# A two-layer decoder trunk: other seven-product units in the MLP, half-block loads, and pinned loads and forms

## The chip, the cores and the metric

The kernel runs on one core of one Trainium2 chip. The metric is the device time of one execution in microseconds (us). The kernel before took 2167.83 us (median of 3 runs, 2164.54 to 2170.95).

The core has a matrix engine (TensorE, PE in the profile; PEld is its weight load), a vector engine (VectorE, DVE), a scalar engine (ScalarE, ACT), GpSimd (POOL) and the sync engine (SyncE, SP), whose queue issues most DMAs. Each engine works through its own queue in order and waits on semaphores.

## The reference

Two layers (`DEPTH = 2`) act on x of 256 rows (tokens) by 2048 columns, in float32. Only the second half of a layer, the MLP, is touched by the change:

```
x  = x + concat([A, Cv]) @ w_out[l]          # attention and short convolution
hm = rmsnorm(x, mlp_norm_g[l]) @ w_up[l]     # 2048 -> 8192
x  = x + square(relu(hm)) @ w_down[l]        # 8192 -> 2048
```

## The kernel before, in words

**Precision.** A float32 product is made of three products in a faster format: each operand is cut into a high part (`hi`) and a low part (`lo = x - hi`), and hi·hi, hi·lo and lo·hi are summed in PSUM. So each weight tile that arrives by DMA is first worked on by ACT (`whi`, `uhi`, lines 291 and 719) and then by DVE (`wlo`, `ulo`, lines 292 and 720), each on 128x1024 elements.

**Pass 1 of the MLP** (lines 908 to 951) goes over 32 units of 256 hidden columns. For unit i it makes the up product in two columns c, each in two halves kh of the contraction (`up_part`, L856), takes the result out of PSUM (`evict`: ACT `ev` L866, DVE L867), squares it (`square`), and two units later (`LAG = 2`) multiplies it with two blocks of rows of `w_down` for the *left* 1024 output columns. That down product is a 2x2 block product done with seven products instead of eight (L904), which needs sums of the blocks: on the side of the activations four sums S1 to S4 (`in_forms`, L890 to L896), on the side of the weights differences `t` (L754, L757, L758), and hi and lo parts of all (L740, L741: `b1`, `b2`, `t13`, `t24`). I call the weight side the forms of a unit. The raw down weights of a pair come into the tile `draw` (pool `dpool`, 2 buffers, line 727); the `t`, `b2`, `t13` and `t24` tiles have one buffer each, `b1` two.

**Pass 2** (from line 1003) makes the *right* 1024 output columns from stored activations. Twelve units, listed in `SEVEN`, go through seven products again: 21 matmuls, and all their forms. The twenty others (`PLAIN`) go through the ordinary product (L1060): 24 matmuls, with two weight tiles of hi and lo (k = 0 and 1). Plain units' activations were written to DRAM in pass 1 with their hi and lo parts (`plain`, L883) and come back two units at a time as a block `g` (line 955, GpSimd's queue) into one of four buffers that the normalized input `nT` of pass 1 had. The seven-product units' activations (`hid`, L879) come back one at a time into the tile `h` (L806; one buffer) and are summed again.

**What sets the order.** TensorE's order is the program's (`manual_schedule`). Weight tiles are *jobs*; `Weights.take` traces jobs up to three ahead of the product that uses them (`AHEAD = 3`), in an order that `mlp` writes out by hand: in pass 2 the four jobs of a seven-product unit (b1 and b2; t13; the activation sums f; t24) are hung behind jobs of the plain units in front of it (lines 828 to 843). The queues of ACT, DVE, POOL and SP are filled by a planner that works with its own estimates of time: an instruction may stand anywhere that its data and buffers allow. `late(...)` pins an instruction behind what was traced before it on its engine.

**Places that the change touches:** the list `SEVEN` (line 36); the wait of 5 ticks in `Norm.factors` (line 460) before the matmul `rbc` that spreads the norm's ratio (line 462; a tick is a fixed step in the matmul stream, one per four up matmuls); `load_rows` (line 724); `quarters` (line 732), whose `keep` pins the forms of unit 0 in pass 1; the order of jobs (line 830); unit 0 of pass 1, whose two columns share one PSUM tile `up0` of two banks (line 913); `block`, `block(0)`, `block(1)` and the first `load_again` (lines 953 to 959); the place of `block(b + 2)` in pass 2 (line 1039).

## Time and profile before

| | us |
|---|---|
| median of 3 runs | 2167.83 |
| lowest, highest | 2164.54, 2170.95 |
| the profiled execution | 2165.76 |
| its span (first to last instruction) | 2164.0 |
| TensorE busy in the span | 2136.1 |
| VectorE busy | 1710.8 |
| ScalarE busy | 1300.9 |

In layer 0, pass 1 begins at 395.8 us of the span, pass 2 at 912.4, and the next layer's mixer at about 1086; in layer 1, pass 1 begins at 1469.7 and pass 2 at 1984.9.

How to read it: the view of waits says which engine stood idle for whom. A timeline line has start, duration, engine, line of the kernel, operation, output tile and inputs, and in brackets the idle time just before it and who ended it. A window line has its bounds and length and then, for each engine, busy time and instructions, the granted TensorE clock, the share of time the DMA engines moved data, and their GB/s. A busy engine is not an engine at its peak: DVE operations overlap a little at their ends, so that the spacing of starts is the better price.

### The profile page before, as it was taken

The page shows a single profiled execution, that of the slowest core. Times are in us where ns is not written, and L with a number is a line of the kernel's source. Part 1 is how long each engine was busy: PE and PEld are TensorE (multiplying, and loading weights), DVE is VectorE, ACT ScalarE, POOL GpSimd, SP SyncE. Part 2 cuts the span into 40 slices and gives each one's busy share as a digit, 9 for nine tenths or more (in the row PEclk, how much of TensorE's full clock was granted, in tenths as well). Part 3 has the DMA queues.
Part 4 walks back from the last instruction along what each step waited for, and adds up shares of the span by engine and source line. Part 5 has one row for each costly group of instructions (what it writes and reads, how often), then busy time and mean ns, then how long its engine had stood idle before and what let it go on. Part 6 is the DMA issues. An engine that isn't in the chain of part 4 may idle for free.

```text
span 2164.0 us, 29108 instructions
## 1 busy us (share of the span) xinstructions
PE 2136.1 (99%) x10966; PEld 1812.7 (84%) x10966; DVE 1710.8 (79%) x2397; ACT 1300.9 (60%) x1760; POOL 166.2 (8%) x246
## 2 busy tenths in 40 slices
PE   9999999999999999999999999999999999999999
PEld 7888888888888888788788888888888888887877
DVE  5677655698888888799866776557988888887997
ACT  6556445566666666656565664446666666665554
POOL 3021200000000000000001222000000000000000
PEclk9999999999999999999999999999999999999999
DMA  7655766587767777887565557656777767778873
GB/s 256 183 158 166 236 187 188 160 263 217 227 216 231 224 224 223 272 288 275 188 184 176 156 166 245 186 172 196 253 227 219 224 216 232 222 224 274 310 271 108
DMA packets 285534, 467.62 MB, mean 216 GB/s; under 512 B 10611, under 2 KB 191429, under 8 KB 282832
## 3 DMA queue, kind: packets, MB, share of 16 engines
q1 hardware_dynamic: 268128, 413.17, 61.2%
q0 software_dynamic: 17216, 52.56, 7.0%
q8 instruction: 86, 1.41, 0.3%
q14 instruction: 56, 0.46, 0.1%
q10 hardware_dynamic: 48, 0.02, 0.0%
HBM read 436.32 MB, written 29.38 MB: 215 GB/s over the span
## 4 chain that ended last, share of the span: by engine, by line
PE 85%; DVE 7%; DMA 4%; issue 2%; ACT 1%; POOL 1%; DVEq 0%; POOLq 0%; ACTq 0%
PE upc L856 30%; PE pr L904 13%; PE o L361 8%; PE rt L1060 5%; PE gb L383 4%; PE v L361 4%; PE ci L383 4%; PE gc L383 4%; PE rt L904 3%; PE q L361 3%; PE k L361 3%; DVE wlo L292 2%; DMA draw<-in_w_down_dram 1%; DMA h<-hid 1%; PE upw L856 1%
## 5 line engine op out<-in xcount | busy, mean ns | idle before, releaser
L291 ACT ACTIVATE whi<-raw 128x1024 fp32r<-128x1024 f32 (+1 forms) x338 | 355.6, 1054 | 410.6 <-PE rt L1060 87.8
L292 DVE TENSOR_TENSOR wlo<-raw,whi 128x1024 fp32r<-128x1024 f32 (+1 forms) x338 | 414.4, 1229 | 237.3 <-ACT whi L291 232.7
L856 PE MATMUL upc<-nT,uhi 128*128 128x512 f32 x1920 | 477.6, 391 | 0.0
L719 ACT ACTIVATE uhi<-uraw 128x1024 fp32r<-128x1024 f32 x256 | 271.2, 1060 | 288.1 <-PE upc L856 254.2
L856 PEld LDWEIGHTS upc<-nT,uhi 128*128 128x128 f32 x1920 | 352.8, 188 | 68.2
L720 DVE TENSOR_TENSOR ulo<-uraw,uhi 128x1024 fp32r<-128x1024 f32 x256 | 313.0, 1223 | 115.7 <-ACT uhi L719 113.3
L856 PEld LDWEIGHTS upc<-nT,ulo 128*128 128x128 f32 x1920 | 261.9, 190 | 18.7
L856 PE MATMUL upc<-nT,ulo 128*128 128x256 f32 x1920 | 267.7, 282 | 0.0
L1060 PE MATMUL rt<-whi,g 128*128 128x512 f32 x608 | 194.0, 393 | 0.0
L361 PE MATMUL o<-whi,cat 128*128 128x512 f32 x512 | 159.6, 390 | 0.0
L1060 PEld LDWEIGHTS rt<-whi,g 128*128 128x128 f32 x608 | 115.7, 190 | 24.1
L1060 PE MATMUL rt<-wlo,g 128*128 128x512 f32 x304 | 120.3, 396 | 9.4 <-DVE wlo L292 9.2
L361 PEld LDWEIGHTS o<-whi,cat 128*128 128x128 f32 x512 | 96.1, 188 | 19.7
L754 DVE TENSOR_TENSOR t<-draw 128x1024 f32<-128x1024 f32 x84 | 102.4, 1219 | 11.0 <-DMA draw<-in_w_down_dram 10.8
L740 ACT ACTIVATE b2h<-draw 128x1024 fp32r<-128x1024 f32 x84 | 88.9, 1058 | 34.6 <-PE pr L904 25.9
L896 DVE TENSOR_TENSOR f<-h,f 128x1024 fp32r<-128x1024 f32 (+1 forms) x88 | 105.2, 1196 | 0.2 <-ACT f L895 0.2
L741 DVE TENSOR_TENSOR t13l<-t,t13h 128x1024 fp32r<-128x1024 f32 x84 | 102.8, 1224 | 2.0 <-ACT t13h L740 0.5
L741 DVE TENSOR_TENSOR t24l<-t,t24h 128x1024 fp32r<-128x1024 f32 x84 | 102.4, 1219 | 0.6 <-ACT t24h L740 0.2
L741 DVE TENSOR_TENSOR b2l<-draw,b2h 128x1024 fp32r<-128x1024 f32 x84 | 102.4, 1219 | 0.4 <-ACT b2h L740 0.3
L361 PE MATMUL o<-wlo,cat 128*128 128x512 f32 x256 | 99.6, 389 | 0.0
L895 ACT ACTIVATE f<-h 128x1024 fp32r<-128x1024 f32 (+1 forms) x88 | 90.4, 1027 | 9.4 <-DVE h L893 9.2
L740 ACT ACTIVATE t24h<-t 128x1024 fp32r<-128x1024 f32 x84 | 88.4, 1052 | 9.6 <-DVE t L758 6.4
(359 smaller groups left out, 3841.9 us busy)
## 6 DMA issues: line engine op xcount, KB each, us to landing
uraw<-in_w_up_dram SPq DMA_DIRECT2D x128, 1024.0 KB, 6.5
raw<-in_w_in_dram SPq DMA_DIRECT2D x191, 512.0 KB, 4.0
draw<-in_w_down_dram SPq DMA_DIRECT2D x88, 1024.0 KB, 5.4
raw<-in_w_down_dram SPq DMA_DIRECT2D x40, 1024.0 KB, 5.6
raw<-in_w_out_dram SPq DMA_DIRECT2D x64, 512.0 KB, 3.6
plain<-f POOLq DMA_DIRECT2D x40, 512.0 KB, 6.5
g<-plain POOLq DMA_DIRECT2D x20, 1024.0 KB, 8.3
hid<-h POOLq DMA_DIRECT2D x24, 256.0 KB, 5.5
```

The lines of the kernel that those rows point to most:

```text
L291: a = nc.scalar.activation(hi[:, k], raw[:, k], AF.Copy)
L292: d = nc.vector.tensor_sub(lo[:, k], raw[:, k], hi[:, k].bitcast(F32))
L361: nc.tensor.matmul(acc[:, t], a.ap[:, pa, k % KG, t * P:(t + 1) * P], (hi, lo)[pw][:, j], start=(k == 0 and n == 0), stop=(k == nk - 1 and ...
L383: nc.tensor.matmul(acc[:, f, 0] if part else acc[:, f], wt[:, k % 4, fs], a.ap[:, 0, k % KG] if part else a.ap[:, :, k % KG], start=(part ...
L719: nc.scalar.activation(hi, src, AF.Copy)
L720: nc.vector.tensor_sub(lo, src, hi.bitcast(F32))
L740: keep(nc.scalar.activation(hi, src, AF.Copy))
L741: keep(nc.vector.tensor_sub(lo, src, hi.bitcast(F32)))
L856: nc.tensor.matmul(acc[:, 0] if part else acc, wt[:, k], a.ap[:, 0, k % KG] if part else a.ap[:, :, k % KG], start=(part == 0 and kh == 0 ...
L896: nc.vector.tensor_sub(f[:, 1, :n], h[:, :n], f[:, 0, :n].bitcast(F32))
L904: nc.tensor.matmul(prods[n], f[:, pa, a], b[pw], start=(start and m == 0), stop=(stop and m == 2))
L1060: nc.tensor.matmul(prods[p], blocks[b][:, slot, pa, 2 * k + t], w[pw][:, n], start=(i == PLAIN[0] and k == 0 and m == 0), stop=False)
```

## The change

- `SEVEN` becomes 5, 7, 9, 11, 13, 15, 18, 20, 22, 24, 26, 28, so that pass 2 begins with five plain units instead of four, and then has two runs of six seven-product units with one plain unit between neighbours and two plain units (16, 17) between the runs.
- The jobs of the first seven-product unit of pass 2 all hang behind the last plain job in front of it, and its forms are pinned (`keep = late`).
- The loads of the down rows of units 0 and 1 in pass 1 are pinned.
- The `rbc` matmul of the MLP's norm comes after 9 ticks instead of 5.
- The two columns of unit 0 in pass 1 get a PSUM tile each.
- A block of activations is loaded in two halves; block 1, the first `h` and the blocks b + 2 are asked for later in the program.

```diff
-SEVEN = (4, 6, 8, 11, 13, 15, 17, 19, 22, 24, 26, 28)
+SEVEN = (5, 7, 9, 11, 13, 15, 18, 20, 22, 24, 26, 28)
...
-                yield 5
+                yield 9
...
-                nc.sync.dma_start(
+                load = nc.sync.dma_start(
...
+                if i < 2 and not col:
+                    late(load)
                 return raw
...
-                keep = late if i == 0 and col == 0 else lambda ins: None
+                keep = late if i == (SEVEN[0] if col else 0) else lambda ins: None
...
                 js = [where[i] + k for k in (1, 2, 0, 3)]
+                if i == SEVEN[0]:
+                    before = [before[-1]] * 4
...
-                    two = mm.tile([P, 2, CH], F32, tag="mm2", name="up0")
-                    two = [two[:, c].rearrange("p (h s) -> p h s", h=2) for c in range(2)]
+                    two = [mm.tile([P, 2, CH], F32, tag="mm2", name=f"up{c}")[:, 0].rearrange(
+                        "p (h s) -> p h s", h=2) for c in range(2)]
...
-                nc.gpsimd.dma_start(blocks[b], plain[b])
+                for s in range(2):
+                    nc.gpsimd.dma_start(blocks[b][:, s], plain[b][:, s])
 
             block(0)
-            block(1)
-            load_again(SEVEN[0])
...
-                if slot == 0 and b + 2 < len(plain):
+                if slot == 0 and b == 0:
+                    block(1)
+                if slot == 1 and b + 2 < len(plain):
                     block(b + 2)
+                if slot == 1 and b == 0:
+                    load_again(SEVEN[0])
```

## The prediction

> **What bounds the kernel now.** First the page, for the shares, then the view of waits for TensorE alone.

> ```profile
> span 2164.0 us, 29108 instructions
> PE 2136.1 (99%) x10966; PEld 1812.7 (84%) x10966; DVE 1710.8 (79%) x2397; ACT 1300.9 (60%) x1760; POOL 166.2 (8%) x246
> ```

> TensorE is idle for 27.9 us of the span. The change leaves its 10966 matmuls alone, so nearly all that can be won lies in those 27.9 us and in stretches at a lower clock. Who holds it up:

> ```profile
> PE rt L1060 <- DVE wlo L292: 9.2, 4, 2.8
> PE rt L904 <- DVE f L896: 3.3, 2, 1.8
> PE up L856 <- ACT ev L866: 2.3, 2, 1.6
> PE rbc L462 <- DVE diag L459: 1.1, 2, 0.5
> ```

> Columns: total us, times, longest. Each falls once or twice per layer. The first is the start of pass 2, the second its end, the others the start of pass 1. The edits stand at exactly these places. Next, windows over pass 2 of layer 0:

> ```profile
> 905.00:925.00 20.00, 15.57 (x61) 12.04 (x60) 14.66 (x19) 8.93 (x11) 0.71 (x1) 0.91 0.94 326
> 920.00:925.00 5.00, 4.75 (x14) 3.77 (x15) 5.00 (x9) 0.44 (x1) 0.00 (x0) 0.66 0.92 355
> 945.00:1060.00 115.00, 113.24 (x500) 93.46 (x499) 108.66 (x139) 69.60 (x73) 2.12 (x4) 1.00 0.76 264
> ```

> After bounds and length: busy time of PE, PEld, DVE, ACT, POOL; then the granted clock, DMA share, GB/s. The start loses 4.4 us of TensorE to idleness and then runs 5 us at a clock of 0.66 (1.7 us lost). In the steady part VectorE is busy 108.7 of 115 us: it is the next limit. Then the timelines of TensorE at both starts of pass 2 (first plain matmul, the two that waited, first seven-product matmul; then first and last of these for layer 1) and of VectorE and SP:

> ```profile
> 912.37 0.39 PE L1060 MATMUL rt<-whi,g 128*128 128x512 f32 x1
> 914.38 0.50 PE L1060 MATMUL rt<-wlo,g 128*128 128x512 f32 x1 [1.62 <-DVE wlo L292]
> 920.25 0.50 PE L1060 MATMUL rt<-wlo,g 128*128 128x512 f32 x1 [2.81 <-DVE wlo L292]
> 941.17 0.39 PE L904 MATMUL rt<-b1h,f 128*128 128x512 f32 x1
> 1984.87 0.39 PE L1060 MATMUL rt<-whi,g 128*128 128x512 f32 x1
> 2014.03 0.39 PE L904 MATMUL rt<-b1h,f 128*128 128x512 f32 x1
> ```

> ```profile
> 898.23 0.37 SPq L727 DMA_DIRECT2D draw<-in_w_down_dram  x1
> 911.97 1.23 DVE L754 TENSOR_TENSOR t<-draw 128x1024 f32<-128x1024 f32 x1 [5.23 <-DMA draw<-in_w_down_dram]
> 918.98 1.22 DVE L292 TENSOR_TENSOR wlo<-raw,whi 128x1024 fp32r<-128x1024 f32 x1
> ```

> The planner put the forms of the first seven-product unit (4) ahead of the plain units' `wlo`. The load they need takes 13.7 us (898.23 to 911.97), VectorE stands 5.2 us in front of it, and `wlo` is late twice.

> **Part by part.** *The price of a matmul.* One seven-product unit (21 matmuls) and one plain unit (24):

> ```profile
> 977.21 0.39 PE L904 MATMUL rt<-b1h,f 128*128 128x512 f32 x1
> 987.41 0.39 PE L904 MATMUL rt<-b1h,f 128*128 128x512 f32 x1
> ```

> 10.20 us / 45 = 0.227 us. A plain unit is 5.44 us, a seven-product unit 4.76.

> *Pass 2, what goes.* Four plain units should take 96 x 0.227 = 21.8 us; they took 941.17 - 912.37 = 28.8 us, and 29.2 in layer 1. So 7.0 and 7.4 us are lost there, restarts and slow clock included. With the forms pinned behind the tenth plain weight, nothing in VectorE's queue waits for that load any more, and ACT's and VectorE's plain work can begin at once:

> ```profile
> 907.13 1.06 ACT L291 ACTIVATE whi<-raw 128x1024 fp32r<-128x1024 f32 x1 [1.66 <-PE pr L985]
> ```

> `whi` of the first plain weight was made 5 us before its use, so `wlo` (1.2 us) would be in time. I count both losses as gone: 14.4 us. The lost clock goes with its gaps. [...]

> *What is late next.* Priced by starts that follow each other on a VectorE that never pauses:

> ```profile
> 994.08 1.22 DVE L741 TENSOR_TENSOR t13l<-t,t13h 128x1024 fp32r<-128x1024 f32 x1
> 995.21 1.22 DVE L741 TENSOR_TENSOR t24l<-t,t24h 128x1024 fp32r<-128x1024 f32 x1
> 996.35 0.28 DVE L890 TENSOR_TENSOR h<-h 128x128 f32<-128x128 f32 x1
> 996.55 0.28 DVE L892 TENSOR_TENSOR h<-h 128x128 f32<-128x128 f32 x1
> 1001.17 0.69 DVE L741 TENSOR_TENSOR b1l<-draw,b1h 128x512 fp32r<-128x512 f32 x1
> 1001.77 0.69 DVE L758 TENSOR_TENSOR t<-draw,t 128x512 f32<-128x512 f32 x1
> ```

> 1.13 us for 1024 elements, 0.60 for 512, 0.20 for 128. Forms of a unit: four of 1024, three of 512: 6.3 us. Its f: four of 128 and one of 1024: 1.9. A plain unit's two `wlo`: 2.3. So a seven-product unit with one plain unit costs VectorE 10.5 us against TensorE's 10.2; each such step loses 0.3, five in a run 1.6, and a step with two plain units (15.6 against 12.8) wins 2.9. The new list has two runs of five such steps with one double step between. Before, VectorE had nearly a whole unit in hand at the first seven-product unit, bought by TensorE's stall; now it has not. Call the first plain matmul P. The pinned forms follow the tenth plain weight, whose buffer (of three) comes free when 84 matmuls are done: P + 19.0, plus 1.1 on ACT and 1.2 on VectorE: P + 21.4. The pins add no wait for data, since that load was there at 911.97; behind them in both queues stand unit 6's weights, needed at P + 32. From there to the end of the last seven-product unit's forms VectorE has 12 x 6.3 + 10 x 1.9 + 12 x 2.3 = 122 us (two f can be made earlier, in idle time): ready at P + 143.6 plus its pauses. TensorE reaches that unit at 27.2 + 11 x 4.76 + 12 x 5.44 = P + 144.9, and its last forms 3.4 us (15 matmuls) later. The pauses:

> ```profile
> DVE h L890 <- DMA h<-hid: 5.2, 6, 1.2
> 1056.43 0.50 PE L904 MATMUL rt<-b1h,f 128*128 128x512 f32 x1 [1.76 <-DVE f L896]
> ```

> With pauses of 5.2 us the stall is 143.6 + 5.2 - 148.3 = 0.5 us if the weight forms are last, 3.9 if f is last; the second row shows f last. I take 3.5 us per layer, between 0 and 9 (pauses doubled, f last). So pass 2 wins 7.0 + 1.8 - 3.5 = 5.3 us in layer 0 and 7.4 + 1.5 - 3.5 = 5.4 in layer 1: 10.7.

> *Blocks, first h.* In the program block 3 belonged to the third plain unit, yet:

> ```profile
> 899.41 1.06 POOL L955 DMA_DIRECT2D g<-plain  x2 [1.67 <-PE upc L856]
> ```

> blocks 2 and 3 were issued together 13 us before pass 2 began, as soon as buffers were free. A later place in the program will not hold them. Halving costs two issues of 0.53 us instead of one on a POOL queue that has nothing else; the cover is the 13 us until use, and without it one issue, 0.5 us, would show. I count 0; a gain from less crowding is possible, but nothing waits for it now. The first `h` also goes when its buffer is free: 0.

> *Start of pass 1.*

> ```profile
> 395.61 10.46 DMA uraw<-in_w_up_dram
> 395.99 1.29 DVE L685 TENSOR_TENSOR x<-o,x 128x512 f32<-128x512 f32 x2 [0.40 <-PE o L361]
> 407.75 2.11 PE L856 MATMUL up<-nT,uhi 128*128 128x512 f32 x8 [1.57 <-ACT ev L866]
> ```

> Column 1's second half waits for the eviction of column 0, which shares its tile; the eviction stood on ACT behind a conversion that waited for `uraw`, 10.5 us in transit beside two `draw` loads. Two tiles end the wait: 1.6 and 0.7 us. The second tile's buffer is still read by the adds that end at 397.28, but column 1 starts after 16 matmuls of column 0: covered; uncovered, 1.7 us. `rbc` four ticks (16 matmuls, some 3.6 us) later ends its two waits of 0.5; what needs the ratio comes much later. Sum: 3.3 us.

> Against it, the pinned loads. Unit 0's was already behind the same `uraw`: 0. Unit 1's now stands behind the up weights of unit 3:

> ```profile
> 427.28 1.84 SPq L712 DMA_DIRECT2D uraw<-in_w_up_dram  x2
> 432.57 0.37 SPq L727 DMA_DIRECT2D draw<-in_w_down_dram  x1
> 439.78 0.63 ACT L740 ACTIVATE b1h<-draw 128x512 fp32r<-128x512 f32 x1 [1.07 <-DMA draw<-in_w_down_dram]
> 444.23 0.40 PE L904 MATMUL pr<-b1h,f 128*128 128x512 f32 x1
> ```

> It goes at about 427.8 instead of before 400, and beside three other loads takes 7.2 us (432.57 to 439.78) or, more crowded, 10: there at 435 to 438. Its forms (6.3 us less the tail that is needed later) must be ready at 444.2, or 442.1 if the wins above hold. That is from nothing to 2 us late; I take 1 per layer. Behind it on SP stands only unit 2's `draw`, whose buffer frees 4.8 us later. Net 1.3.

> *Sum.* 10.7 + 1.3 = 12.0 us off the profiled execution's 2165.76 (span 2164.0 and 1.8 around it), 2153.8. That execution lies 2.1 us under the median; the same 12.0 off 2167.83 is 2156.

> **The rivals.**

> (1) *VectorE, not TensorE, sets the end of pass 2.* It was busy without a hole from 911.97, so TensorE's stall was cover, and removing it moves the wait to f and `t24` in the two runs of six. For it: 108.7 of 115 us, and the wait for f at the end. Against: VectorE also idled 5.2 us in front of the load, which is regained. With stalls of 7 us per layer: 1.8 + 1.9 + 1.3 = 5 us won, 2163. It decides when f comes last at every unit.

> (2) *The slow clock stays.* If the slow stretch comes from something other than the gaps, 1.7 us per layer remain: 2159. Against: the clock is 1.00 in the long window without such a gap. [...]

> (3) *The second pair takes the first's place* (slower). Only unit 5's forms are pinned; `b1` has two buffers, so unit 7's first conversion can stand early in ACT's queue.

> ```profile
> 906.76 10.95 SPq L727 DMA_DIRECT2D draw<-in_w_down_dram  x2
> draw<-in_w_down_dram SPq DMA_DIRECT2D x1, 1024.0 KB, 11.5
> ```

> The second load goes at 906.76 and lands 11.5 us later, at 918.3. If the planner puts that conversion ahead of the third plain weight, needed at 912.37 + 5.4 = 917.8, ACT blocks until 918.3, `wlo` is ready at about 921.4: 3.4 us of idleness, 1.7 of slow clock, and with 7.5 in the runs (toward the end of 9) 12.6 per layer against 8.8 lost before. With unit 1's load 2 us late per layer, 2176. It decides from the order on ACT alone; once the conversion stands behind the fourth plain weight it costs nothing. Before, such a conversion stood there, which speaks against it.

> (4) *The change does not do what it says*: the planner satisfies the pins and still puts `t` of another unit first, since only the first unit is bound. `t` has one buffer, which speaks against. Time as before, 2167.

> **How the numbers follow.** Forecast 0.58 (2156); rival 1 0.22 (2163); rival 2 0.06 (2159); rival 3 0.09 (2176); rival 4 0.05 (2167). About 0.3% (6.5 us) is what a measurement can tell from no change, so faster means under 2161.3: forecast and rival 2, 0.64. Within: rivals 1 and 4, 0.27. Slower: 0.09. Range: with no stall in pass 2 and unit 1's load in time the gain is 17.7 + 3.3 = 21 us, 2147; above, it takes in rivals 1 and 4 and stops short of rival 3: 2146 to 2170.

> **What would show it.** Right: no wait of `rt` L1060 for `wlo`; clock 1.00 in the first 20 us of pass 2; first seven-product matmul 27 us after P; waits of L904 for f or `t24l` of 2 to 5 us per layer within the runs of six; no waits of `up` and `rbc`; blocks 0 to 3 still issued before P. Wrong: waits of L904 over 7 us per layer (rival 1), of L1060 for `whi` behind a `b1h` (rival 3), of `pr` in pass 1's unit 3 over 2 us.

## The result, and the profile after

The kernel after takes 2181.3 us (median of 6 runs, 2178.97 to 2182.99), the kernel before 2167.5 us in the same comparison (6 runs, 2164.54 to 2171.33). The ratio is 1.0064, 95% interval 1.0054 to 1.0075: slower by 0.64%. The profiled execution took 2179.71 us, 13.95 more than that of before. Medians here and below are of fast executions; one execution of experiment 8, of 5498.63 us, is left out by this. The page of after begins:

```profile
span 2177.9 us, 29137 instructions
PE 2143.1 (98%) x10966; PEld 1816.0 (83%) x10966; DVE 1712.5 (79%) x2397; ACT 1302.7 (60%) x1760; POOL 175.2 (8%) x266
```

TensorE is idle for 34.8 us instead of 27.9. That is only 6.9 of the 13.9 us of span. The other 7.0 us are *busy* time: the same 10966 matmuls took longer, and the granted clock of the whole execution is 0.995 instead of 0.998. Now the view of waits for TensorE:

```profile
PE rt L908 <- ACT t24h L742: 7.5, 2, 4.4
PE rt L908 <- DVE f L900: 6.6, 6, 1.6
...
PE upc L860 <- ACT ev L870: 1.9, 2, 1.0
PE pr L908 <- DVE t24l L743: 1.9, 2, 0.9
PE pr L908 <- ACT t24h L742: 1.6, 2, 1.2
PE up L860 <- DVE nT L256: 1.5, 2, 0.8
...
PE rt L908 <- ACT f L899: 1.3, 1, 1.3
PE rt L908 <- DVE t24l L743: 1.2, 2, 0.8
```

L908 is the seven-product line (`rt` in pass 2, `pr` in pass 1), L860 the up product, L1067 the plain one. The four waits shown of before are gone but for `f`: no wait for `wlo`, none for `diag`, none of `up` for `ev`. In their place stand waits for `t24` at the first seven-product unit of pass 2, the same for unit 0 of pass 1, and more for `f`. The stages, each from the start of its first matmul to that of the next stage (pass 2 to the end of its last seven-product matmul), with layer 0 / layer 1:

| us | before | after |
|---|---|---|
| up to pass 1 | 395.8 | 396.6 |
| pass 1 | 516.6 / 515.2 | 519.8 / 517.8 |
| pass 2, plain units in front | 28.8 / 29.2 | 27.2 / 27.2 |
| pass 2, from the first seven-product unit on | 130.1 / 129.8 | 136.2 / 134.2 |

At 0.227 us per matmul the last two rows should be 21.8 and 127.9 before (four plain units in front) and 27.2 and 122.4 after (five). So the start of pass 2 is at its ideal now, 7.0 and 7.4 us regained, but behind it 13.8 and 11.8 us are lost where it was 2.2 and 1.9. TensorE is idle for 8.5 and 8.1 us of that; the rest is matmuls that took longer. And pass 1 got longer by 3.2 and 2.6.

**First unit of pass 2.** TensorE's wait, and VectorE's timeline in front of it (the unit's first form, `b1l`, its last `t` and `t24l`, and some of what stands between):

```profile
943.60 0.39 PE L908 MATMUL rt<-b1h,f 128*128 128x512 f32 x1
951.87 0.80 PE L908 MATMUL rt<-t24h,f 128*128 128x512 f32 x1 [4.41 <-ACT t24h L742]
```

```profile
937.87 0.68 DVE L743 TENSOR_TENSOR b1l<-draw,b1h 128x512 fp32r<-128x512 f32 x1
...
940.75 0.68 DVE L743 TENSOR_TENSOR b1l<-draw,b1h 128x512 fp32r<-128x512 f32 x1
941.35 1.22 DVE L900 TENSOR_TENSOR f<-h,f 128x1024 fp32r<-128x1024 f32 x1
942.49 2.35 DVE L292 TENSOR_TENSOR wlo<-raw,whi 128x1024 fp32r<-128x1024 f32 x2
...
946.49 1.22 DVE L292 TENSOR_TENSOR wlo<-raw,whi 128x1024 fp32r<-128x1024 f32 x1
948.49 0.29 DVE L894 TENSOR_TENSOR h<-h 128x128 f32<-128x128 f32 x1 [0.79 <-DMA h<-hid]
...
950.04 0.68 DVE L760 TENSOR_TENSOR t<-draw,t 128x512 f32<-128x512 f32 x1
...
951.85 1.22 DVE L743 TENSOR_TENSOR t24l<-t,t24h 128x1024 fp32r<-128x1024 f32 x1 [0.59 <-ACT t24h L742]
```

The forms start at 937.87, 21.5 us after pass 2 began (916.40). But ten strangers stand between its seven forms (unit 7's `b1l`, `b2l` and `f`, three `wlo`, four sums of `h`), and the last form ends at 953.07, 15.2 us after the first. A pin keeps an instruction behind what was traced before it; it does not keep others out. Meanwhile VectorE had had room: in these windows over the plain units of before and of after the third busy time is VectorE's,

```profile
912.37:941.17 28.80, 24.30 (x97) 18.93 (x96) 28.00 (x38) 14.66 (x16) 0.55 (x1) 0.94 0.81 280
```

```profile
916.40:943.60 27.20, 27.20 (x122) 22.53 (x120) 22.93 (x31) 15.34 (x16) 2.13 (x4) 1.00 0.93 316
```

0.8 us idle before, 4.3 us after.

**The clock.** Windows of 3.413 us over this stall, at the same phase as every other half-clock stretch of the trace (after the five busy times: granted clock):

```profile
946.13:949.54 3.41, 1.33 (x5) 0.75 (x5) 2.62 (x5) 0.83 (x1) 0.00 (x0) 1.00 0.90 335
949.54:952.96 3.42, 0.80 (x1) 0.29 (x1) 2.79 (x5) 1.06 (x1) 0.00 (x0) 0.50 0.32 73
952.96:956.37 3.41, 3.25 (x8) 2.60 (x9) 3.31 (x5) 1.63 (x3) 0.00 (x0) 0.50 0.64 259
956.37:959.78 3.41, 3.41 (x17) 2.79 (x16) 3.41 (x4) 2.92 (x4) 0.00 (x0) 1.00 0.83 257
```

Here each window in which TensorE was busy for 1.33 us or less is followed by one at half clock, and the one with 3.25 us is not; I estimate the cost of a half-clock window at half of TensorE's busy time in it, up to 1.7 us of its 3.41. Leaving out the end of the program, where TensorE has run out of work, before has 2 such windows, after 6, with 6.7 and 17.6 us of busy time: 5.4 of the 7.0 us of longer busy time by this estimate.

**Start of pass 1.** SyncE's issues, ACT, and TensorE, in the kernel after:

```profile
426.38 0.37 SPq L712 DMA_DIRECT2D uraw<-in_w_up_dram  x1
426.80 0.57 SPq L727 DMA_DIRECT2D draw<-in_w_down_dram  x1
427.85 0.37 SPq L712 DMA_DIRECT2D uraw<-in_w_up_dram  x1
```

```profile
435.14 1.06 ACT L719 ACTIVATE uhi<-uraw 128x1024 fp32r<-128x1024 f32 x1 [3.44 <-DMA uraw<-in_w_up_dram]
436.11 1.04 ACT L742 ACTIVATE t24h<-t 128x1024 fp32r<-128x1024 f32 x1
```

```profile
437.20 0.50 PE L908 MATMUL pr<-t24h,f 128*128 128x512 f32 x1 [1.16 <-ACT t24h L742]
441.04 3.63 PE L860 MATMUL upc<-nT,uhi 128*128 128x512 f32 x8 [0.96 <-ACT ev L870]
```

The pinned load of unit 1 (`draw`) is issued 0.4 us behind an up load and 1.1 us ahead of the next. ACT waits for the first of these up loads until 435.14, 8.8 us after its issue, and behind that in its queue stands `t24h` of unit 0. The pinned load itself is in time: `b1h` of unit 1 starts at 438.00 and does not wait for it. The 8 up matmuls at 441.04 take 3.63 us, where they take 2.00 in experiment 1 below: the granted clock is 0.50 from 440.96 to 444.37 us.

### The profile page after: what moved, and what is told of

Read it like the earlier page. It is cut to its first block, busy times and chain, and to the rows that moved or that the text cites. A ratio compares the mean times of both kernels' runs of the same rounds, so it can differ in the third digit from the quotient of the medians.

```text
span 2177.9 us, 29137 instructions
## 1 busy us (share of the span) xinstructions
PE 2143.1 (98%) x10966; PEld 1816.0 (83%) x10966; DVE 1712.5 (79%) x2397; ACT 1302.7 (60%) x1760; POOL 175.2 (8%) x266
## 4 chain that ended last, share of the span: by engine, by line
PE 85%; DVE 6%; DMA 4%; issue 2%; ACT 1%; POOL 1%; ACTq 0%; DVEq 0%; POOLq 0%
PE upc L860 30%; PE pr L908 13%; PE o L361 8%; PE rt L1067 5%; PE gb L383 4%; PE v L361 4%; PE ci L383 4%; PE gc L383 3%; PE q L361 3%; PE k L361 3%; PE rt L908 3%; DMA h<-hid 2%; DVE wlo L292 1%; PE upw L860 1%; PE pr L988 1%
## 5 line engine op out<-in xcount | busy, mean ns | idle before, releaser
L292 DVE TENSOR_TENSOR wlo<-raw,whi 128x1024 fp32r<-128x1024 f32 (+1 forms) x338 | 414.6, 1229 | 253.9 <-ACT whi L291 249.3
L291 ACT ACTIVATE whi<-raw 128x1024 fp32r<-128x1024 f32 (+1 forms) x338 | 356.0, 1054 | 408.2 <-PE rt L1067 78.2
L860 PE MATMUL upc<-nT,uhi 128*128 128x512 f32 x1920 | 479.3, 392 | 1.9 <-ACT ev L870 1.9
L860 PEld LDWEIGHTS upc<-nT,uhi 128*128 128x128 f32 x1920 | 353.7, 189 | 71.2 <-ACT ev L870 2.8
L860 PEld LDWEIGHTS upc<-nT,ulo 128*128 128x128 f32 x1920 | 262.0, 190 | 18.8
L860 PE MATMUL upc<-nT,ulo 128*128 128x256 f32 x1920 | 267.7, 282 | 0.0
L1067 PE MATMUL rt<-whi,g 128*128 128x512 f32 x608 | 192.4, 390 | 0.0
L361 PE MATMUL o<-whi,cat 128*128 128x512 f32 x512 | 159.6, 390 | 0.0
L1067 PEld LDWEIGHTS rt<-whi,g 128*128 128x128 f32 x608 | 114.9, 189 | 24.0
L1067 PE MATMUL rt<-wlo,g 128*128 128x512 f32 x304 | 118.8, 391 | 0.0
L742 ACT ACTIVATE b2h<-draw 128x1024 fp32r<-128x1024 f32 x84 | 89.0, 1060 | 41.5 <-PE pr L908 29.2
L361 PEld LDWEIGHTS o<-whi,cat 128*128 128x128 f32 x512 | 96.1, 188 | 19.8
L361 PE MATMUL o<-wlo,cat 128*128 128x512 f32 x256 | 99.6, 389 | 0.0
L742 ACT ACTIVATE t24h<-t 128x1024 fp32r<-128x1024 f32 x84 | 88.5, 1054 | 15.7 <-DVE t L760 11.6
L742 ACT ACTIVATE t13h<-t 128x1024 fp32r<-128x1024 f32 x84 | 88.5, 1054 | 11.7 <-DVE t L756 7.2
## 6 DMA issues: line engine op xcount, KB each, us to landing
uraw<-in_w_up_dram SPq DMA_DIRECT2D x128, 1024.0 KB, 6.5
draw<-in_w_down_dram SPq DMA_DIRECT2D x88, 1024.0 KB, 5.4
raw<-in_w_down_dram SPq DMA_DIRECT2D x40, 1024.0 KB, 6.2
```

The costliest lines, as they stand in the source:

```text
L291: a = nc.scalar.activation(hi[:, k], raw[:, k], AF.Copy)
L292: d = nc.vector.tensor_sub(lo[:, k], raw[:, k], hi[:, k].bitcast(F32))
L361: nc.tensor.matmul(acc[:, t], a.ap[:, pa, k % KG, t * P:(t + 1) * P], (hi, lo)[pw][:, j], start=(k == 0 and n == 0), stop=(k == nk - 1 and ...
L742: keep(nc.scalar.activation(hi, src, AF.Copy))
L860: nc.tensor.matmul(acc[:, 0] if part else acc, wt[:, k], a.ap[:, 0, k % KG] if part else a.ap[:, :, k % KG], start=(part == 0 and kh == 0 ...
L1067: nc.tensor.matmul(prods[p], blocks[b][:, slot, pa, 2 * k + t], w[pw][:, n], start=(i == PLAIN[0] and k == 0 and m == 0), stop=False)
```

## The experiments

Ratios are to the kernel before on the same chip, with 95% intervals. Stages of all of them, in us (pass 2 from its first matmul to the end of the last seven-product one; half-clock windows as above):

| kernel | median | ratio | pass 1 | pass 2 | half-clock |
|---|---|---|---|---|---|
| before | 2168.1 to 2168.6 (2167.5 beside after) | 1 | 516.6 / 515.2 | 158.9 / 159.0 | 2 |
| after | 2181.3 | 1.0064 [1.0054, 1.0075] | 519.8 / 517.8 | 163.4 / 161.4 | 6 |
| 1 loads unpinned | 2175.4 | 1.0034 [1.0022, 1.0046] | 514.9 / 515.0 | 167.8 / 161.5 | 5 |
| 2 hung two earlier | 2175.8 | 1.0036 [1.0023, 1.0049] | 520.2 / 517.8 | 159.9 / 158.5 | 4 |
| 3 forms unpinned | 2189.9 | 1.0093 [1.0075, 1.0111] | 525.9 / 523.5 | 160.6 / 157.5 | 8 |
| 4 list of before | 2179.5 | 1.0049 [1.0036, 1.0061] | 520.1 / 518.4 | 162.0 / 163.7 | 7 |
| 5 hung six earlier | 2174.0 | 1.0030 [1.0018, 1.0042] | 520.0 / 518.4 | 155.1 / 161.4 | 4 |
| 6 two earlier, two `h` | 2160.1 | 0.9965 [0.9952, 0.9979] | 519.2 / 518.1 | 154.8 / 151.8 | 3 |
| 7 before, two tiles, 9 ticks | 2166.8 | 0.9993 [0.9985, 1.0002] | 515.1 / 515.4 | 158.3 / 160.5 | 2 |
| 8 unpinned, four earlier | 2168.9 | 1.0003 [0.9993, 1.0012] | 514.9 / 515.1 | 163.0 / 157.7 | 4 |
| 9 unpinned, four earlier, two `h` | 2147.5 | 0.9904 [0.9891, 0.9917] | 513.5 / 514.5 | 150.9 / 150.9 | 1 |
| 10 after, two `h` | 2161.9 | 0.9968 [0.9956, 0.9980] | 517.4 / 516.4 | 156.7 / 156.1 | 5 |
| 11 before, two `h` | 2167.4 | 0.9997 [0.9989, 1.0006] | 515.0 / 514.7 | 160.4 / 159.4 | 5 |
| 12 before, list of after | 2178.7 | 1.0062 [1.0044, 1.0079] | 517.3 / 515.8 | 165.6 / 160.9 | 3 |

My theory at first: three losses, the pinned load (pass 1), the forms hung too late (first unit of pass 2), and VectorE's lead used up in the runs of six (late `f`).

**1. Loads not pinned** (after, less two lines).

```diff
-                if i < 2 and not col:
-                    late(load)
```

> The kernel after, with the pin on the down-row loads of units 0 and 1 in pass 1 taken off; all else of the change stays. Theory: the pinned load of unit 1 travels beside the up weights of unit 3, both land late, and pass 1 loses 2.5 us of idleness per layer to t24 and the late eviction, and about 2 us to the slow clock behind them. Then this kernel's load goes before 400 us again, the waits of pr for t24h and t24l and of upc for ev are gone, pass 1 of layer 0 takes 515 to 516 us instead of 519.8, and the median is 2171 to 2174. Rival A: pass 1 is longer because the up tiles and the 9 ticks moved other work (nT, the norm's sums): pass 1 stays at 519 and the median at 2179 to 2182. Rival B: the regained time is lost again in pass 2, whose VectorE work is later than TensorE's: pass 1 shorter, pass 2 longer by as much, 2179 to 2182.

Pass 1 came down by 4.9 and 2.8 us, as the theory has it; the waits of unit 0's `t24` were 0.2 us in layer 0 and none in layer 1. ACT's row that stood at 435.14 is now:

```profile
432.01 1.06 ACT L719 ACTIVATE uhi<-uraw 128x1024 fp32r<-128x1024 f32 x1 [1.09 <-DMA uraw<-in_w_up_dram]
```

The up load that it waits for was issued at 425.61, so it took 6.4 us instead of 8.8. With the pin gone, the load of unit 1 no longer travels beside it; that the sharing of the DMA engines is what held it up fits these two times, but no run separates it from the rest of the pin. The median is higher than expected by 1.4 us, because pass 2 of layer 0 gave 4.4 back, in waits for `f` (6.6 us instead of 3.6) and in slower matmuls (TensorE is busy for 9.2 us of the half-clock windows at 945.39, 948.81 and 1061.45 us; in after for 7.5 us of its three in that pass): rival B in one layer of two.

**2. The forms hung two weights earlier** (after).

```diff
-                    before = [before[-1]] * 4
+                    before = [before[-3]] * 4
```

> The kernel after, with the four jobs of the first seven-product unit hung behind the last plain job but two (two weights earlier) instead of the last; they stay pinned. Theory: the pin holds the forms back but does not keep other work out between them, so from the last plain job they need 15.2 us instead of the 7.5 I counted; two weights are 24 matmuls, 5.4 us, more than the 4.9 us of waiting for t24. Then the waits of L908 for t24h and t24l at the first seven-product unit are under 1 us, the slow clock behind them is gone, and of the 7.5 and 6.0 us lost there 10 to 13 come back: 2168 to 2172. Rival A: VectorE's total work sets the end of pass 2, and the time won at the first seven-product unit is lost as waits for f in the last three: 2178 to 2182. Rival B: the forms, earlier, push a plain wlo out: waits of L1067 of 3 us or more per layer, 2174 to 2180.

The wait for `t24` is gone, but for 0.4 us at the third unit; only 6.4 us came back in pass 2, and `f` is late in its place, in layer 0 at the fifth unit:

```profile
989.01 0.50 PE L908 MATMUL rt<-b1h,f 128*128 128x512 f32 x1 [2.30 <-ACT f L899]
991.84 0.72 PE L908 MATMUL rt<-b1h,f 128*128 128x512 f32 x1 [2.10 <-DVE f L900]
```

Late hanging is shown; that what is won is lost again a few units later looked like rival A.

**3. The forms of the first unit not pinned** (after).

```diff
-                keep = late if i == (SEVEN[0] if col else 0) else lambda ins: None
+                keep = late if i == 0 and col == 0 else lambda ins: None
```

> The kernel after, with the forms of the first seven-product unit of pass 2 no longer pinned; the jobs are hung as in the change. Theory: without the pin the planner puts the first t in front of the plain weights again, VectorE waits there for the load, and the waits of L1067 for wlo return (4 to 9 us for both layers with the slow clock behind them), while the waits for t24 at the first seven-product unit (8.7 us in both layers, 13.5 with the clock) go: the place of the stall moves back and the time falls by 3 to 8 us, 2173 to 2178. Rival: the load is there in time now, because pass 1 is later, and nothing waits at either place: 2166 to 2170. If the hanging and not the pin made the stall, t24 is still late: 2180 to 2183.

The time lies above all three ranges. The planner does put `t` in front again and VectorE does wait for its load, but here it is not a `wlo` of pass 2 that stands behind it first, it is an `f` that pass 1's last products need:

```profile
915.56 1.23 DVE L756 TENSOR_TENSOR t<-draw 128x1024 f32<-128x1024 f32 x1 [4.73 <-DMA draw<-in_w_down_dram]
916.70 0.69 DVE L900 TENSOR_TENSOR f<-h,f 128x512 fp32r<-128x512 f32 x1
```

```profile
917.44 1.07 PE L988 MATMUL pr<-whi,f 128*128 128x512 f32 x2 [3.86 <-DVE f L900]
```

Pass 1 grew by 6.1 and 5.7 us, pass 2 shrank by 2.8 and 3.9. The waits for `wlo` are 0.4 and 0.5 us. So without the pin the stall moves into pass 1, and the pin is worth having, 5 us by these stages (8.6 by the medians); what cost is how late the forms are hung.

**4. The list of before in the kernel after.**

```diff
-SEVEN = (5, 7, 9, 11, 13, 15, 18, 20, 22, 24, 26, 28)
+SEVEN = (4, 6, 8, 11, 13, 15, 17, 19, 22, 24, 26, 28)
```

> The kernel after, with the list of seven-product units of the kernel before (4, 6, 8, 11, 13, 15, 17, 19, 22, 24, 26, 28); pins and hanging stay, now for unit 4. Theory: the two runs of six use up VectorE's lead, and the last three units lose about 6 us in layer 0 and 4 in layer 1 to late f; the list of before has a pause of two plain units after each three to five and loses 1.8 and about 1.5 there. The stall for t24 at the first seven-product unit stays, since the hanging is the same. So 2172 to 2176. Rival A: the late f comes from the stall ahead of it (VectorE's queue is late from there), and stays with any list: 2179 to 2182. Rival B: with four plain units in front instead of five there is 5.4 us less time before the first forms, and the stall for t24 grows by as much: 2180 to 2190.

Pass 2 takes 162.0 / 163.7: no better, and the waits for `f` are 3.1 and 5.8 us where the kernel after has 3.6 and 4.3. The time is rival A's (2179 to 2182): with the forms hung this late, `f` is late with either list. The interval overlaps that of after, so even the 1.8 us are not sure.

**5. Hung six weights earlier** (after; `[j for j in mine if j < where[i]][-7]` in place of `before[-1]`).

> The kernel after, with the four jobs of the first seven-product unit hung six weights earlier than in the change (behind the seventh last plain job in front of it, not the last); they stay pinned. Theory: what counts is VectorE's lead. In the change it stands idle for 7.8 us of the first 35 us of pass 2 and has no lead when the run of six begins; started six weights earlier, the forms fill those holes. Then t24 is not late at the first unit, and the late f of the run, 5.9 and 6.3 us of waits in layer 0 and layer 1 with two hung two weights earlier, falls under 2 us per layer: pass 2 from its first matmul to the last seven-product one takes 154 to 157 us instead of 163.4 and 161.4; 2166 to 2171. Rival A: f is late because its load waits for the one buffer of h, and the lead does not matter: f stays late by 4 us or more per layer, 2173 to 2177, as with two weights earlier. Rival B: so early, the forms push plain wlo out, as in the kernel before: waits of L1067 over 2 us per layer, 2174 or more.

Layer 0 gained 8.3 us in pass 2 and came into the theory's range there (155.1), layer 1 gained none. But the waits for `f` are 3.6 and 6.6 us instead of under 2, and the time is in rival A's range: an earlier start of the forms does not cure a late `f`. That spoke against my third reason, without settling it, as layer 0 shows.

**6. Two buffers for `h`**, on top of experiment 2.

```diff
-                again[i] = fpool.tile([P, 8, P], F32, tag="h", name="h", bufs=1)
+                again[i] = fpool.tile([P, 8, P], F32, tag="h", name="h", bufs=2)
...
-                h = fpool.tile([P, 8, P], F32, tag="h", name="h", bufs=1)
+                h = fpool.tile([P, 8, P], F32, tag="h", name="h", bufs=2)
```

> The kernel with the jobs hung two weights earlier (2175.8), and two buffers for h instead of one, in both passes. Theory of the lead: in the 35 us before the late f VectorE has no hole worth 1 us, so a load that comes earlier changes nothing there: f stays late by 4 us or more in layer 0 around the fourth or fifth seven-product unit, 2174 to 2178. Rival: the load of h goes only when the last f is made, and that is what makes f late: with two buffers f is no longer late at that unit, and 5 to 7 us come back over both layers, 2168 to 2171.

My theory lost by 14 us. No wait of pass 2 for `f` is left, and 15.7 us came back by the medians, 11.8 of them in pass 2: the rival, and more than the 5 to 7 us that I had put on it. What remains there are waits for `t24l`, 3.9 and 1.1 us. The loop is in the trace of after, one turn of it on VectorE, and on SyncE's queue the load:

```profile
982.60 1.22 DVE L900 TENSOR_TENSOR f<-h,f 128x1024 fp32r<-128x1024 f32 x1
990.96 0.29 DVE L894 TENSOR_TENSOR h<-h 128x128 f32<-128x128 f32 x1 [1.93 <-DMA h<-hid]
...
993.84 0.28 DVE L897 TENSOR_TENSOR h<-h 128x128 f32<-128x128 f32 x1
996.31 1.22 DVE L900 TENSOR_TENSOR f<-h,f 128x1024 fp32r<-128x1024 f32 x1
```

```profile
983.84 0.34 SPq L808 DMA_DIRECT2D h<-hid  x1
```

The load of the next `h` can go only when `f` has read the last one: 1.2 us to the issue, 7.1 to the first sum, 5.4 through the sums to `f`: 13.7 us. The 11 `f` of pass 2 from 941.35 to 1072.60 in layer 0 stand 13.1 us apart on the mean, where TensorE takes 10.7 (nine steps of 10.2 us and one, with two plain units, of 15.6). This lag does not show at once: the second `f` was ready at 942.6, some 19 us before TensorE used it (961.3), and TensorE first waits for an `f` at the tenth unit (1049.9). VectorE is busy for 123.3 of the 136.2 us meanwhile, because the planner fills the loop's gaps with later units' forms; that made it look like the limit.

**7. Two tiles and 9 ticks, alone** (before, with the two hunks of the diff for line 460 and unit 0).

> The kernel before, with two parts of the change alone: a PSUM tile for each column of unit 0, and 9 ticks instead of 5. Theory: these are worth what pass 1 gained when the load's pin was off, 1.7 us in layer 0 and 0.2 in layer 1 (a new wait of 0.75 for nT eats part of the 1.6 and 0.7 that go): 2 us less than the kernel before, 2165 to 2166.5. Rival A: they lose as much as they win: 2167 to 2168.5. Rival B (as I forecast): 3.3 us less, 2164 to 2165.

The interval holds 1: not told apart from no change. By stages pass 1 is 1.5 shorter and 0.2 longer. A wait for `nT` of 0.75 per layer takes the place of those that went.

**8. Loads unpinned and forms hung four weights earlier** (after; `[-5]` in the line of experiment 5).

> The kernel after without the pin on the down-row loads, and with the jobs of the first seven-product unit hung four weights earlier than in the change. Theory: the two losses are at different places and add: 5.9 us for the loads, and 8 to 12 us for the place of the forms, so 2163 to 2168, at or below the kernel before, and pass 1 takes 515 us in both layers. Rival: what is won at the start of pass 1 is lost again in pass 2 as VectorE is the limit there: 2169 to 2173.

The time lies between the two ranges; the stages tell more. Pass 1 is as forecast, and pass 2 of layer 0 still takes 163.0 with 8.1 us of waits for `f`. That is the rival, but not for its reason: mended ahead of it, the time is lost again at `f`, and experiment 9 shows that the buffer of `h` is the cause.

**9. All three mends** (experiment 8 with the diff of experiment 6).

> The kernel after with three mends: no pin on the down-row loads, the first seven-product unit's jobs hung four weights earlier than in the change, and two buffers for h. Theory: the three losses (the shared load in pass 1, the late t24, the loop of f through one buffer) are separate. With the stages as they were measured one at a time: 395.8 + 514.9 + 27.3 + 125 + 398.5 + 515.1 + 27.3 + 124 + 20.1 = 2148 us of span, 2148 to 2153 as a median, under both kernels. Rival: what is won in pass 1 is lost in pass 2, as with the first two mends alone, because VectorE is the limit there: 2157 to 2161.

2147.5 us, half a us under the range, 0.96% under the kernel before and 33.8 us under the kernel after. Its page, and VectorE's `f` in the run of six:

```profile
PE 2132.0 (99%) x10966; PEld 1811.9 (84%) x10966; DVE 1713.9 (80%) x2397; ACT 1313.4 (61%) x1760; POOL 175.3 (8%) x266
```

```profile
956.51 1.22 DVE L898 TENSOR_TENSOR f<-h,f 128x1024 fp32r<-128x1024 f32 x1
965.73 1.22 DVE L898 TENSOR_TENSOR f<-h,f 128x1024 fp32r<-128x1024 f32 x1
976.50 1.22 DVE L898 TENSOR_TENSOR f<-h,f 128x1024 fp32r<-128x1024 f32 x1
986.53 1.22 DVE L898 TENSOR_TENSOR f<-h,f 128x1024 fp32r<-128x1024 f32 x1
```

One each 10.0 us: VectorE, with 1.4 us more to do in all than in the kernel after, keeps step with TensorE. Pass 2 takes 150.9 of an ideal 149.6.

**10. The kernel after with two buffers for `h`** (the diff of experiment 6 alone).

> The kernel after with two buffers for h and nothing else. Theory: t24 stays late at the first seven-product unit (4 to 5 us of waits and a slow stretch per layer), the late f of the runs goes: f made every 10.5 to 11.5 us in the run of six instead of every 12.8. 3.6 and 4.3 us of waits and the slow stretch of layer 0 come back, and little more: 2169 to 2174. Rival: the stall for t24 is itself behind h's sums in VectorE's queue, and goes too: 2160 to 2165. Second rival: f was late for VectorE's total work, and two buffers helped only because the jobs were hung earlier as well: 2178 to 2181.

The time is in the first rival's range; the stages lie between it and the theory. 12.0 us came back in pass 2: the waits for `f` are gone, and that for `t24h` at the first unit is 2.0 and 1.9 us, no longer 4.4 and 3.1, since `f` of unit 7 and the next sums no longer stand in front of it on VectorE. What stays, 11.0 us against experiment 9 in pass 2, is the late hanging, and whatever the loads' pin does to pass 2.

**11. The kernel before with two buffers for `h`.**

> The kernel before with two buffers for h and nothing else. Theory: its list breaks the runs after three, five and four seven-product units, so the loop of f costs it only 1.8 and 1.5 us of waits; these go, the 14 us at the start of pass 2 (the wait for wlo behind t) stay: 2164 to 2166.5. Rival A: the loop also fed the wait at the start of pass 2 or pass 1's order, and more comes back: 2158 to 2163. Rival B: a load of h more in flight makes the load that t waits for later: 2168.5 or more.

No change by the interval, 0.9 us above my range, and not for the reason I gave. The seven-product part reaches its ideal (128.0 / 128.0), but more work now stands behind the `t` that waits for its load, and the plain part takes 32.4 / 31.4:

```profile
922.62 0.80 PE L1060 MATMUL rt<-wlo,g 128*128 128x512 f32 x1 [5.97 <-DVE wlo L292]
```

**12. The new list, alone** (before, with line 36 of the diff).

> The kernel before with the change's list of seven-product units and nothing else. Theory of the loop: f is made every 12.8 us against steps of 10.2 us, so two runs of six lose more than runs of three, five and four: 2 to 4 us more of waits for f per layer, with a slow stretch where they are close together, and the wait for wlo at the start stays: 2171 to 2177. Rival: the list costs nothing by itself (as it hardly did when the list of before was put into the kernel after: 1.8 us), 2166 to 2169.5.

```profile
PE rt L1060 <- DVE wlo L292: 8.9, 7, 2.9
PE rt L904 <- DVE f L896: 8.7, 8, 2.2
```

10.6 us slower by the medians, 1.7 above my range: with the stall at the start still there (8.9), the runs of six add 5.4 us of waits for `f` (8.7 against 3.3 before). With one buffer for `h` the new list by itself costs nearly what the whole change does; with two, and the other two mends, it runs 1.3 us from its ideal (experiment 9). Experiments 4 and 12 together say that the list of before is spared late `f` only with its own early hanging; why in that pair alone, no run shows.

## Why the prediction was wrong

The step that failed is the account of VectorE in pass 2. It let the pinned forms run as one block, so that their stall was in no term, and it priced the late `f` by VectorE's total work. In place of that the runs showed forms with other work between them, 15.2 us instead of 6.3, and a loop through the one buffer of `h`, 13.1 us a turn against 10.7 us of TensorE. A second term, the pinned load in pass 1, was priced for the wrong reader.

**The waits for `wlo` go: right.** The plain part is 27.2 us in both layers, and no wait of L1067 is left. 14.4 us were counted as regained, and were. Experiment 3 shows what the pin does in this: without it VectorE stands 4.73 us in front of the load again, and the stall comes back, mostly at the end of pass 1.

**"The pinned forms follow the tenth plain weight ... P + 21.4": right, and the step behind it wrong.** They start at P + 21.5. I then let VectorE run 6.3 us of forms in one block, to P + 27.7. They needed 15.2 us, to P + 36.7, against a use at about P + 30.6. The stall (4.4 + 0.5, and 3.1 + 0.8 in layer 1) appears in no term of my sum.

**"I take 3.5 us per layer" for the end of pass 2: cause wrong, and the size right by luck.** The waits for `f` are 3.6 and 4.3 us. But I had added up VectorE's work, and the tempo was set by the loop through the one buffer of `h`. I had quoted its row ("DVE h <- DMA h<-hid") and booked it as pauses of 5.2 us in all, not as a loop that must turn once per unit. The same work with two buffers keeps step. Rival 1, VectorE as the limit, is refuted by experiments 6 and 9, although the sign set for it came: TensorE waits 8.5 and 8.1 us on the seven-product line, over the 7 per layer.

**Start of pass 1, "net 1.3": wrong.** I priced the pinned load of unit 1 for its own forms (0 to 2 us) and not for what it does to the up load beside it, and so to unit 0's `t24h` behind that on ACT: the pin cost 4.9 and 2.8 us (experiment 1). The wins were 1.9 by experiment 1 against before, 1.3 by experiment 7, instead of 3.3: the wait moved to `nT`.

**The clock: half right.** It was 1.00 in the plain units (916.40 to 943.60 us) once their gaps were gone. I took a slow stretch as something that goes with a gap removed, and put no such price on the new ones: four more windows, 5.4 us by the estimate above. One of them, at 14 us of the span, has nothing to do with the change: of the kernels made from before, 11 and 12 have it and 7 does not; of those made from after, 10 does not. These are single executions; the last section shows that window in before and in after.

**Blocks and first `h` at 0: nothing speaks against it.** Blocks 0 to 3 were still issued before pass 2, the last two here; no wait falls on them.

```profile
903.43 2.13 POOL L960 DMA_DIRECT2D g<-plain  x4 [0.61 <-PE upc L860]
```

**Rivals 3 and 4 did not happen:** there is no wait for `whi` in pass 2, and the order did change as the pins say.

**The sum.** Forecast -12.0, measured +13.9 in the profiled executions. Pass 2: -10.7 forecast, +6.9 measured. Pass 1: -1.3 forecast, +5.8 measured. The rest, 1.2, is mostly the window at 14 us.

What stays open: why, with one buffer, pass 2 of layer 0 lost 4.4 more in experiment 1, why the two layers differ by 6 in experiment 5, and why the list of before has few waits for `f` in the kernel before and not in experiment 4. The start of each turn of the loop depends on where the planner puts six or seven instructions; I did not take that apart further.

## What to carry to other kernels

Before costing a faster schedule by an engine's total work, look for each single-buffered tile and add up its loop (load, use, release, next load); here the loop of `h` set the tempo although VectorE looked full. A pin says what an instruction stands behind, not what may come between, so chains that must run together have to be started with room for strangers. And a load that is held back is to be priced also by the loads that it then travels beside, not only by who reads it: here an up load took 8.8 us beside it and 6.4 with the pin gone.

## What the runs showed of the hardware

```profile
9.86:13.28 3.42, 1.70 (x9) 1.09 (x7) 0.97 (x2) 2.52 (x7) 0.52 (x1) 1.00 1.06 399
13.28:16.69 3.41, 2.96 (x16) 2.34 (x17) 3.04 (x5) 3.06 (x5) 0.00 (x0) 1.00 1.03 347
```

and in after so:

```profile
10.88:14.29 3.41, 1.25 (x6) 0.46 (x4) 1.61 (x4) 3.04 (x8) 0.00 (x0) 1.00 1.06 383
14.29:17.70 3.41, 3.41 (x11) 2.84 (x12) 3.24 (x5) 1.67 (x3) 0.00 (x0) 0.50 1.00 345
```
